# Retention in a two-layer hybrid decoder on one Trainium2 core: the later queries meet the first 256 keys through one state matrix per head

## The chip, the cores and the metric

The kernel runs on one core of one Trainium2 chip. The metric is the device time of one execution in microseconds (us); lower is better. The profile comes from one execution of the same program, recorded by the hardware profiler. The engines are TensorE (PE for its matmuls, PEld for its weight loads), VectorE (DVE), ScalarE (ACT), GpSimd (POOL) and SyncE (SP, which issues most of the DMAs).

## The reference, cut to what matters

Two decoder layers over 16 meta tokens and 512 real ones (T = 528, width 1024). In each layer one projection feeds eight heads of forgetting attention (FoX) of 64 columns and four retention heads of 128. The heads' outputs are concatenated, projected and added to the stream; a SwiGLU block follows. For a retention head:

```python
o_t = sum_{s<=t} gamma_h^(t-s) (q_t.k_s) v_s        # gamma_h = 1 - 2**(-5-h)
q, k = rotate(rq), rotate(rk) * 128**-0.5
y = (o - mean(o)) * rsqrt(var(o) + EPS) * g          # over the head's 128 columns
ret_out = silu(rg) * y
```

The sum over s can be taken key by key, as scores and then products, or for a group of keys at once: the matrix sum_s gamma^(c-s) k_s v_s^T is a state of 128x128, and a query t >= c meets it with the weight gamma^(t-c). Both give the same o.

## The kernel before

Everything is held transposed, 128 features on the partitions and the 528 tokens in the free dimension. Each fp32 operand is split into a high and a low half in the format fp32r (`split`, L149: a copy by ScalarE at L150, a subtraction by VectorE at L151), and each product is three matmuls: high x high, high x low, low x high. In layer 0 all tokens are computed, in layer 1 (`real`) only the queries of the 512 real ones.

A retention head is a list of steps made by `ret_steps` (L671). `values` (L677) transposes the values on TensorE, subtracts each key's mean over the head's columns (so the group norm needs no mean later) and splits them into `rvh`, `rvl`. `scores` (L699) takes a group of key blocks of 128 keys: offsets 0, 128, 256, 384 and a last block of 16 keys at 512. It loads the head's decay table `dec` (128 x 528) once by SyncE (L702, one buffer for all heads), multiplies keys by all queries that come after the block's first key (L722), multiplies the result out of PSUM by the decays (L727, `sd`) and splits it into `rsh`, `rsl`; the block of 16 goes to a small tile `re` (L735 to L737). `product` (L741) multiplies values by scores into one PSUM bank `po` of 512 columns (L756, the block of 16 at L753), in layer 0 the 16 meta columns into a bank of their own (L761, copied at L762); behind the last block ScalarE copies `po` to `d` (L764) and the squares for the norm are taken. `weigh`, `head_norm` and `gate` finish the head; its result `mxh`, `mxl` feeds the output projection.

The groups are {0}, {1} and {2, 3, 4} (L800), so a head has three steps of scores and three of products. Widths of the score matmuls in layer 0: twice 264, 400, 272, 144 and 16 columns; in layer 1: 512, 400, 272, 144 and 16.

The order on TensorE is written out by hand (L1349): the plan is one list of steps, and TensorE executes it in that order. The base of a stretch is the dense projections, one step for each 128 input features (`dense_steps`, L205: six matmuls of 264 columns or three of 512; L225). Between its steps are merged (`merge`, L254) the steps of one pair of attention heads (scores at L519, turns by transposes at L429, products at L589) and those of the retention heads, at places given as numbers of base steps (`ret_places`, L1321, called for heads 0 and 1 each in a stretch of its own, for heads 2 and 3 in one together). With `f` for the list of a head's steps, the ten places go to values, scores of 0, scores of 1, product of 0, scores of 2-4, product of 1, product of 2-4, weigh, norm and gate. The order of the instructions on the other engines follows from a scheduler that goes by the order of the program and by what is ready. The weights of a projection are fetched by SyncE into three buffers (L166) some steps ahead and cast and split by ScalarE with VectorE or GpSimd (L199, L202).

## Time and profile before

| | before |
|---|---|
| device time, median of 3 runs | 1268.74 us (1267.4 to 1270.0) |
| the profiled execution's own time | 1268.53 us |
| its span, first to last instruction | 1266.7 us |
| TensorE busy / its weight loader busy | 1251.2 us (99%) / 1194.1 us (94%) |
| VectorE busy | 991.9 us (78%) |
| ScalarE busy | 704.8 us (56%) |
| GpSimd busy | 273.3 us (22%) |

The span is what the profile covers; the 1.8 us between it and the execution's time lie around it. Busy shares are means over the whole span. Matmuls overlap in the array, so the sum of their durations is no measure of TensorE's time; the distance from one start to the next is. A wait is put down to what came last before the waiting instruction.

### The profile page before, as it was taken

To read this page: it belongs to the slowest core of one execution; us is meant where nothing else is said; L and a number is where in the kernel's file an instruction comes from. 1 tells how busy PE (TensorE), PEld (TensorE's weight loads), DVE (VectorE), ACT (ScalarE), POOL (GpSimd) and SP (SyncE) were. 2 spreads that over 40 slices of the span, in tenths; PEclk is the share of its full clock that TensorE was granted. 3 is DMA by queue.
4 is the path that set the end of the run, shared out by engine and by line. 5 is a ranking of instruction groups with operands and counts; after the bars stand their busy time and mean duration, and the time that the engine had idled before them with its cause. 6 is when DMAs were issued, how large, how long until landed. Compare 5 with 4: busy or idle time off the path is not lost.

```text
span 1266.7 us, 23526 instructions
## 1 busy us (share of the span) xinstructions
PE 1251.2 (99%) x9225; PEld 1194.1 (94%) x9225; DVE 991.9 (78%) x1804; ACT 704.8 (56%) x1301; POOL 273.3 (22%) x539
## 2 busy tenths in 40 slices
PE   9999999999999999999999999999999999999997
PEld 8899999999999999999999989998789999999996
DVE  8887756779988888887786877567899888888867
ACT  6766655676444444444466766557764444444445
POOL 3455546420000000000126556554100000000000
PEclk9999999999999999999999999999999999999999
DMA  6122222223333333332322122222223333333321
GB/s 218 50 76 75 76 77 72 72 67 118 104 97 100 100 101 100 101 101 84 101 77 84 60 86 74 70 90 67 100 94 123 100 101 101 100 101 101 100 84 67
DMA packets 43342, 116.19 MB, mean 92 GB/s; under 512 B 5088, under 2 KB 12000, under 8 KB 43232
## 3 DMA queue, kind: packets, MB, share of 16 engines
q1 hardware_dynamic: 42800, 114.41, 28.1%
q8 instruction: 72, 1.18, 0.4%
q14 instruction: 38, 0.31, 0.1%
q10 hardware_dynamic: 432, 0.29, 0.1%
HBM read 112.58 MB, written 2.10 MB: 91 GB/s over the span
## 4 chain that ended last, share of the span: by engine, by line
PE 93%; ACT 3%; DVE 3%; issue 1%; DMA 0%; ACTq 0%; DVEq 0%
PE psd L225 30%; PE psa L907 18%; PE psd L1042 14%; PE psd L907 13%; PE psa L225 5%; PE psa L1042 4%; PE psa L429 2%; PE psa L519 2%; PE psa L589 1%; PE psa L756 1%; PE psa L722 1%; ACT whi L199 1%; PE psa L298 0%; ACT xh L327 0%; DMA raw<-w_in 0%
## 5 line engine op out<-in xcount | busy, mean ns | idle before, releaser
L202 POOL TENSOR_TENSOR wlo<-raw,whi 128x128 fp32r<-128x128 f32 x504 | 258.2, 548 | 260.1 <-ACT whi L199 259.7
L225 PE MATMUL psd<-xh,whi 128*128 128x264 f32 (+1 forms) x792 | 195.5, 314 | 0.2 <-DVE tq L442 0.2
L225 PE MATMUL psd<-xl,whi 128*128 128x264 f32 (+1 forms) x792 | 186.7, 303 | 0.6 <-DVE xl L328 0.6
L225 PE MATMUL psd<-xh,wlo 128*128 128x264 f32 (+1 forms) x792 | 187.0, 304 | 0.0
L225 PEld LDWEIGHTS psd<-xh,whi 128*128 128x128 f32 x792 | 128.6, 189 | 5.0 <-issue 0.6
L225 PEld LDWEIGHTS psd<-xh,wlo 128*128 128x128 f32 x792 | 127.2, 188 | 6.2 <-DVE wlo L202 0.4
L225 PEld LDWEIGHTS psd<-xl,whi 128*128 128x128 f32 x792 | 127.8, 189 | 5.4 <-DVE xl L328 1.4
L199 ACT CAST whi<-raw 128x512 fp32r<-128x512 f32 (+1 forms) x168 | 97.9, 613 | 41.5 <-PE psd L225 28.4
L895 ACT CAST whi<-raw 128x1024 fp32r<-128x1024 f32 (+2 forms) x62 | 54.9, 885 | 51.3 <-PE psd L907 39.8
L895 ACT CAST fwhi<-raw 128x1024 fp32r<-128x1024 f32 (+2 forms) x62 | 55.6, 897 | 47.5 <-PE psd L907 40.0
L122 POOL MEMSET kc<- 64x528 f32 x2 | 1.1, 533 | 345.4 <-PE psa L907 345.4
L896 DVE TENSOR_TENSOR wlo<-raw,whi 128x1024 fp32r<-128x1024 f32 (+2 forms) x62 | 62.9, 1014 | 12.7 <-ACT whi L895 12.6
L896 DVE TENSOR_TENSOR fwlo<-raw,fwhi 128x1024 fp32r<-128x1024 f32 (+2 forms) x62 | 64.0, 1032 | 11.1 <-ACT fwhi L895 10.9
L907 PE MATMUL psa<-th,whi 128*128 128x264 f32 (+1 forms) x232 | 65.4, 282 | 0.0
L907 PE MATMUL psa<-th,wlo 128*128 128x264 f32 (+1 forms) x232 | 65.4, 282 | 0.0
L907 PE MATMUL psa<-tl,whi 128*128 128x264 f32 (+1 forms) x232 | 65.3, 282 | 0.0
L907 PE MATMUL psa<-th,fwhi 128*128 128x264 f32 (+1 forms) x224 | 63.4, 283 | 0.0
L907 PE MATMUL psa<-tl,fwhi 128*128 128x264 f32 (+1 forms) x224 | 63.3, 283 | 0.0
L907 PE MATMUL psa<-th,fwlo 128*128 128x264 f32 (+1 forms) x224 | 63.2, 282 | 0.0
L536 ACT ACTIVATE pr<-pr,nmax 128x144 f32<-128x144 f32 (+1 forms) x64 | 36.8, 576 | 45.4 <-DVE nmax L523 26.1
L895 ACT CAST fwhi<-S 128x1024 fp32r<-128x1024 f32 x20 | 21.0, 1049 | 68.6 <-PE psa L907 66.5
L973 ACT COPY e<-psa 128x264 f32<-128x264 f32 (+1 forms) x114 | 42.8, 376 | 28.4 <-PE psa L907 24.1
(365 smaller groups left out, 4041.2 us busy)
## 6 DMA issues: line engine op xcount, KB each, us to landing
raw<-w_in SPq DMA_DIRECT2D x54, 512.0 KB, 3.5
raw<-w_gate SPq DMA_DIRECT2D x44, 512.0 KB, 3.9
fraw<-w_up SPq DMA_DIRECT2D x38, 512.0 KB, 3.5
raw<-w_down SPq DMA_DIRECT2D x64, 256.0 KB, 2.9
raw<-w_out SPq DMA_DIRECT2D x16, 512.0 KB, 3.4
raw<-w_down SPq DMA_DIRECT2D x32, 192.0 KB, 2.5
raw<-w_up SPq DMA_DIRECT2D x6, 512.0 KB, 3.5
h<-x_t SPq DMA_DIRECT2D x8, 264.0 KB, 4.5
```

The source lines that it names most:

```text
L199: pin(nc.scalar.copy(hi, job["raw"][:, c0:c1]), pinned)
L202: pin(sub(lo[:, c:c + step], job["raw"][:, c0 + c:c0 + c + step], hi[:, c:c + step].bitcast(F32)), pinned)
L225: nc.tensor.matmul(ps[1][b][:, 0:c1 - c0], w[:, wk, :], x[:, c0:c1], start=(k == 0 and i == 0), stop=(k == n - 1 and i == 2))
L429: nc.tensor.transpose(ps[:, 128 * j:128 * j + 128], src[:, o:o + 128], idt)
L519: nc.tensor.matmul(sc[0:nq, 0:c1 - c0], qq[:, q0:q0 + nq], kk[:, c0:c1], start=(i == 0), stop=(i == 1))
L536: nc.scalar.activation(pr, pr, AF.Exp, bias=nmax[0:nq], scale=-1.0, accum_out=rsum)
L589: nc.tensor.matmul(po[:, c0:SEQ], v[:, j, :], pp[:, j, META + c0:T], start=(j == 0 and i == 0), stop=(j == 4))
L895: nc.scalar.copy(hi, src)
L896: nc.vector.tensor_sub(lo, src, hi.bitcast(F32))
L907: nc.tensor.matmul(bank()[:, 0:b.shape[-1]], a[:, o + k, :], b, start=(fresh and k == 0 and i == 0), stop=(k == n - 1 and i == 2), skip_gr ...
L973: nc.scalar.copy(self.t["e"][:, i], self.t["x"][:, 0:w])
L1042: nc.tensor.matmul(v[:, 0:c1 - c0], a[:, s * n + k, :], b[:, c0:c1], start=(k == 0 and i == 0), stop=(k == n - 1 and i == 2))
```

## The change

Queries from token 256 on (`CUT`) no longer meet key blocks 0 and 1 one by one. `scores` takes blocks 0 and 1 only against queries below 256 (256 and 128 columns; 240 and 128 in layer 1), both in one PSUM bank, and blocks 2 to 4 as before. A new step `keys` transposes the rotated keys of blocks 0 and 1 (kept in fp32 in a tile of their own, `rkf`) on TensorE, weights each key with its decay up to token 256 and splits them. A new step `memory` multiplies them with the centred values to the state, six matmuls of 128 columns, and splits it. `product` of the second group begins with three matmuls of the state by the queries from 256 on (272 columns). The decays in the table for blocks 2 to 4 are now those of the key alone; the query's factor is multiplied on at the end, by VectorE out of PSUM into columns 256 on of `d`, in place of a copy by ScalarE; the first 240 real columns are copied by ScalarE once block 1 is done. A head has ten steps as before, now values, scores of 0-1, keys, memory, scores of 2-4, product of 0-1, product of 2-4, weigh, norm and gate, and they take the same ten places in this order. The decay table is 962 columns wide.

```diff
@@ -33,6 +33,9 @@
 GAMMA = tuple(1.0 - 2.0 ** (-5 - h) for h in range(RH))
 NEG = -1.0e30
 HALF = T // 2
+CUT = 256
+DOFF = (0, 0, CUT, T, 2 * T - CUT - 128)
+DEC = DOFF[4] + META + T - CUT + 2
 PSTEP = 416
 
 
...
@@ -630,13 +633,15 @@
                 nc.scalar.copy(sv(xsw, rl, 0, 64), pv(ps, rl, 64, 128))
                 nc.scalar.copy(sv(xsw, rl, 64, 128), pv(ps, rl, 0, 64))
                 nc.vector.tensor_mul(sv(xsw, rl), sv(xsw, rl), sv(ly["sr"], rl))
-                t1 = tt("tq")
+                t1 = at("rkf", F32) if nm == "rk" else tt("tq")
                 nc.vector.tensor_mul(sv(t1, rl), pv(ps, rl), sv(ly["cr"], rl))
                 nc.vector.tensor_add(sv(t1, rl), sv(t1, rl), sv(xsw, rl))
                 th = at(nm + "h")
                 tl = at(nm + "l")
                 split(sv(th, rl), sv(tl, rl), sv(t1, rl))
                 st[nm] = (th, tl)
+                if nm == "rk":
+                    st["rkf"] = t1
             return go
 
         def v_done(ps):
...
@@ -692,36 +697,32 @@
                     nc.vector.tensor_sub(vh[64:128, 4], c[64:128, 0], vl[64:128, 4].bitcast(F32))
             st["rv"] = (vh, vl)
 
-        def q_start(j):
-            return max(qlo, KOFF[j] if j < 4 else SEQ)
+        def q_range(j):
+            return max(qlo, KOFF[j]), (CUT if KOFF[j] < CUT else T)
 
 
         def scores(grp):
             if grp[0] == 0:
-                dec = at("dec", F32, (128, T), 1)
+                dec = at("dec", F32, (128, DEC), 1)
                 nc.sync.dma_start(dec, decay[hd])
                 st["dec"] = dec
             dec = st["dec"]
             (qh, ql), (kh, kl) = st["rq"], st["rk"]
             sd = tt("sd")
             used = 0
-            ps = None
+            ps = psum_a()
             reads = []
             for j in grp:
-                q0 = q_start(j)
-                d0 = q0 - KOFF[j]
-                n = T - q0
+                q0, q1 = q_range(j)
+                d0 = DOFF[j] + q0 - KOFF[j]
+                n = q1 - q0
                 kn = KLEN[j]
-                for c0, c1 in (((0, HALF), (HALF, n)) if n > 512 else ((0, n),)):
-                    if ps is None or n > 512:
-                        ps = psum_a()
-                    off = used if len(grp) > 1 else 0
-                    sc = ps[0:kn, off:off + c1 - c0]
-                    ko = KOFF[j]
-                    for i, (a, b) in enumerate(((kh, qh), (kh, ql), (kl, qh))):
-                        nc.tensor.matmul(sc, a[:, ko:ko + kn], b[:, q0 + c0:q0 + c1], start=(i == 0), stop=(i == 2))
-                    reads.append((kn, slice(used + c0, used + c1), sc, slice(d0 + c0, d0 + c1)))
-                kept[j] = (used, grp[0])
+                sc = ps[0:kn, used:used + n]
+                ko = KOFF[j]
+                for i, (a, b) in enumerate(((kh, qh), (kh, ql), (kl, qh))):
+                    nc.tensor.matmul(sc, a[:, ko:ko + kn], b[:, q0:q1], start=(i == 0), stop=(i == 2))
+                reads.append((kn, slice(used, used + n), sc, slice(d0, d0 + n)))
+                kept[j] = used
                 used += n
             for kn, o, sc, dd in reads:
                 nc.vector.tensor_mul(sd[0:kn, o], sc, dec[0:kn, dd])
...
@@ -738,30 +739,56 @@
                 kept["e"] = e
             kept["t", grp[0]] = (sh, sl)
 
+        def keys():
+            (_, n, p3), = transpose_into(st["rkf"], KOFF[0:2])
+            th, tl = (at(f"rt{i}", shape=(128, 2, 128)) for i in "hl")
+            for j in range(n):
+                g = st["dec"][:, DEC - 2 + j:DEC - 1 + j]
+                nc.scalar.activation(th[:, j], p3[:, j], AF.Copy, scale=g)
+                nc.vector.scalar_tensor_tensor(tl[:, j], p3[:, j], g, th[:, j].bitcast(F32), ALU.mult, ALU.subtract)
+            st["kt"] = th, tl
+
+        def memory():
+            (th, tl), (vh, vl) = st["kt"], st["rv"]
+            ps = psum_a()[:, 0:128]
+            for j in range(2):
+                for i, (a, b) in enumerate(((th, vh), (th, vl), (tl, vh))):
+                    nc.tensor.matmul(ps, a[:, j, :], b[:, j, :], start=(j == 0 and i == 0), stop=(j == 1 and i == 2))
+            mh, ml = (at(f"rm{i}", shape=(128, 128)) for i in "hl")
+            split(mh, ml, ps)
+            st["memory"] = mh, ml
+
         def product(grp):
             vh, vl = st["rv"]
             if grp[0] == 0:
                 st["po"] = psum_a()
                 st["d"] = at("d", F32, bufs=2)
             po, d = st["po"], st["d"]
+            sh, sl = kept["t", grp[0]]
+            if grp[0]:
+                (mh, ml), (qh, ql) = st["memory"], st["rq"]
+                for i, (a, b) in enumerate(((mh, qh), (mh, ql), (ml, qh))):
+                    nc.tensor.matmul(po[:, CUT - META:SEQ], a, b[:, CUT:T], start=(i == 0), stop=False)
             for j in grp:
-                used, g0 = kept[j]
-                q0 = q_start(j)
+                used = kept[j]
+                q0, q1 = q_range(j)
                 qa = max(q0, META)
-                sh, sl = kept["t", g0]
                 if j == 4:
                     nc.tensor.matmul(po[:, SEQ - META:SEQ], vh[:, 4, :], kept["e"], start=False, stop=True)
                 else:
                     for i, (a, b) in enumerate(((vh, sh), (vh, sl), (vl, sh))):
-                        nc.tensor.matmul(po[:, qa - META:SEQ], a[:, j, :], b[:, used + qa - q0:used + T - q0],
-                                         start=(j == 0 and i == 0), stop=False)
+                        nc.tensor.matmul(po[:, qa - META:q1 - META], a[:, j, :], b[:, used + qa - q0:used + q1 - q0],
+                                         start=(j == 0 and i == 0), stop=(j == 1 and i == 2))
                 if j == 0 and not real:
                     pm = psum_a()
                     for i, (a, b) in enumerate(((vh, sh), (vh, sl), (vl, sh))):
                         nc.tensor.matmul(pm[:, 0:META], a[:, 0, :], b[:, 0:META], start=(i == 0), stop=(i == 2))
                     nc.scalar.copy(d[:, 0:META], pm[:, 0:META])
+                if j == 1:
+                    nc.scalar.copy(d[:, META:CUT], po[:, 0:CUT - META])
                 if j == 4:
-                    nc.scalar.copy(d[:, META:T], po)
+                    with tc.high_priority():
+                        nc.vector.tensor_mul(d[:, CUT:T], po[:, CUT - META:SEQ], st["dec"][:, DEC - 2 - T + CUT:DEC - 2])
                     sq = tt("sq")
                     if hd == RH - 1:
                         sh, sl = tt("sqh", F32R), tt("sql", F32R)
...
@@ -797,8 +824,9 @@
             split(sv(mh, real), sv(ml, real), sv(d, real))
             st["mix"] = (mh, ml)
 
-        G = ((0,), (1,), (2, 3, 4))
-        return [values] + [lambda g=g: scores(g) for g in G] + [lambda g=g: product(g) for g in G] + [weigh, head_norm, gate]
+        G = ((0, 1), (2, 3, 4))
+        return [values, lambda: scores(G[0]), keys, memory, lambda: scores(G[1]),
+                lambda: product(G[0]), lambda: product(G[1]), weigh, head_norm, gate]
 
     def add_h(m, real):
         def go(ps):
...
@@ -1320,8 +1348,7 @@
 
         def ret_places(hd, *places):
 
-            f = rs[hd]
-            return list(zip(places, (f[0], f[1], f[2], f[4], f[3], f[5], f[6], f[7], f[8], f[9])))
+            return list(zip(places, rs[hd]))
 
         for g in range(2):
             main, rest = fs[g]
...
@@ -1356,12 +1383,17 @@
     ang = np.arange(T, dtype=np.float32)[None, :] * inv[:, None]
     cos, sin = np.cos(ang), np.sin(ang)
     rope = np.stack([np.concatenate([cos, cos], 0), np.concatenate([-sin, sin], 0)]).astype(np.float32)
-    decay = np.zeros((RH, 128, T), np.float64)
+    decay = np.zeros((RH, 128, DEC), np.float64)
     k = np.arange(128)[:, None]
-    q = np.arange(T)[None, :]
     for hd in range(RH):
-        decay[hd] = np.where(q >= k, np.exp(np.maximum(q - k, 0) * math.log(GAMMA[hd])), 0.0)
-    decay = (decay * 128.0 ** -0.5).astype(np.float32)
+        g = math.log(GAMMA[hd])
+        for o, n, base in ((0, CUT, None), (DOFF[2], T - CUT, 0), (DOFF[3], T - CUT - 128, 128), (DOFF[4], META, CUT)):
+            q = np.arange(n)[None, :]
+            power = q - k if base is None else 0 * q - k - base
+            decay[hd][:, o:o + n] = np.where(q >= k, np.exp(np.where(q >= k, power, 0) * g), 0.0) * 128.0 ** -0.5
+        decay[hd][:, DOFF[4] + META:DEC - 2] = np.exp(np.arange(T - CUT)[None, :] * g)
+        decay[hd][:, DEC - 2:] = np.exp((CUT - np.array([[0, 128]]) - k) * g) * 128.0 ** -0.5
+    decay = decay.astype(np.float32)
     mask = np.where(np.arange(128)[None, :] <= np.arange(128)[:, None], 0.0, NEG).astype(np.float32)
     return rope, decay, mask, np.eye(128, dtype=np.float32)
 
```

## Prediction

> **What bounds the kernel now.** I read the page first, then the waits of TensorE and of its weight loader, then the timeline around each retention head, engine by engine.
>
> ```profile
> span 1266.7 us, 23526 instructions
> ...
> PE 1251.2 (99%) x9225; PEld 1194.1 (94%) x9225; DVE 991.9 (78%) x1804; ACT 704.8 (56%) x1301; POOL 273.3 (22%) x539
> ...
> PE 93%; ACT 3%; DVE 3%; issue 1%; DMA 0%; ACTq 0%; DVEq 0%
> ```
>
> TensorE is busy for 99% of the span, its weight loader for 94%, and the chain that ended last is 93% TensorE. So the change is worth what it does to TensorE's stream of instructions, plus what it adds to or takes from TensorE's waits. The retention heads cause few of these:
>
> ```profile
> PE psa L756 <- DVE rsl L151: 0.7, 2, 0.4
> PEld psa L756 <- DVE rsl L151: 1.6, 3, 0.7
> ```
>
> Both rows tell of the same stalls, in which a product waits for the low half of its scores: between 0.7 and 1.6 us, and I take 1.2.
>
> What a matmul costs is not its duration (they overlap) but the distance from its start to the next start:
>
> ```profile
> 215.17 0.28 PE L722 MATMUL psa<-rqh,rkh 128*128 128x264 f32 x1
> ...
> 215.90 0.41 PE L225 MATMUL psd<-xh,whi 128*128 128x264 f32 x2
> ...
> 217.06 0.34 PE L722 MATMUL psa<-rql,rkh 128*128 128x400 f32 x1
> ...
> 217.42 0.40 PE L225 MATMUL psd<-xh,whi 128*128 128x264 f32 x2
> ...
> 220.38 0.29 PE L722 MATMUL psa<-rqh,rkh 128*128 128x272 f32 x1
> ...
> 220.76 0.23 PE L722 MATMUL psa<-rqh,rkh 128*128 128x144 f32 x1
> 220.82 0.28 PE L722 MATMUL psa<-rql,rkh 128*128 128x144 f32 x1
> ```
> ```profile
> 864.77 0.39 PE L722 MATMUL psa<-rqh,rkh 128*128 128x512 f32 x1
> 865.00 0.40 PE L722 MATMUL psa<-rql,rkh 128*128 128x512 f32 x1
> ...
> 872.09 0.71 PE L429 MATMUL psa<-idt,pd 128*128 128x128 f32 x5
> 872.55 0.48 PE L225 MATMUL psd<-xh,whi 128*128 128x512 f32 x1
> 872.87 0.39 PE L225 MATMUL psd<-xl,whi 128*128 128x512 f32 x1
> ```
> ```profile
> 1248.24 0.27 PE L907 MATMUL psa<-ah,whi 128*128 128x240 f32 x1
> ...
> 1249.92 0.28 PE L907 MATMUL psa<-ah,whi 128*128 128x240 f32 x1
> ```
>
> 512 columns take 0.23 us. 400 take 0.36/2 = 0.18, 272 take 0.38/3 = 0.127, 264 take 0.73/6 = 0.122, and 240 take 1.68/15 = 0.112. I put 256 between the last two, at 0.118. Five transposes of 128 columns take 0.46 us, and the matmul behind them takes 0.32 instead of 0.23, so they cost (0.46 + 0.09)/5 = 0.11 each. From 240 columns down to 128 the price hardly falls: below that width I read the loading of a fresh 128x128 weight as the limit. This decides the sum.
>
> **The change, part by part.**
>
> *TensorE's stream, for one head.* Scores of the first two key blocks: in layer 0 they were six matmuls of 264 and three of 400 (6 x 0.122 + 3 x 0.18 = 1.27 us) and become three of 256 and three of 128 (0.35 + 0.33 = 0.68), a gain of 0.59. In layer 1 three of 512 and three of 400 (1.23) become three of 240 and three of 128 (0.67), a gain of 0.56. Products: three of 512 and three of 400 (1.23) become three of 240, three of 128 and three of 272 against the state (0.34 + 0.33 + 0.38 = 1.05), a gain of 0.18. New: two transposes of the keys and six matmuls of 128 columns for the state, 8 x 0.11 = 0.88 us. Key blocks 2, 3 and 4 keep their widths. Net: 0.88 - 0.77 = +0.11 us in layer 0 and 0.88 - 0.74 = +0.14 in layer 1; over four heads each, **+1.0 us** (the last digit of the rows leaves some 0.4 either way). A third of the score columns go, yet the stream gets no shorter, since what goes is wide and what comes is narrow.
>
> [...]
>
> *A wait of the second product.* Accumulator `po` is one bank of 512 columns. The new `product` copies its columns 0 to 240 out on ScalarE after key block 1, and the state's matmuls then write columns 240 to 512 of the same bank. Does TensorE wait for that copy, though the columns differ? The trace has two like cases:
>
> ```profile
> 128.16 0.17 PE L722 MATMUL psa<-rqh,rkl 128*16 128x16 f32 x1
> ```
> ```profile
> 127.53 0.69 DVE L151 TENSOR_TENSOR ptl<-psa,pth 128x512 fp32r<-128x512 f32 x1
> 128.37 0.72 DVE L727 TENSOR_TENSOR sd<-psa,dec 128x272 f32<-128x272 f32 x3
> ```
> ```profile
> L500 ACT CAST vv<-psa 128x256 fp32r<-128x256 f32 x16 | 5.9, 369 | 5.2 <-PE psa L429 2.5 <-DVE vv L501 2.5
> ```
>
> VectorE was free at 128.22 but began on the 272 columns of block 2 only at 128.37, when the 16 columns of block 4 in that bank were done (128.16 + 0.17). And ScalarE's copies at L500 sat idle 2.5 us for VectorE's reads of other columns of their bank. So the program orders accesses by bank, and I expect TensorE's second product, with everything behind it in TensorE's queue (the next projection), to wait for ScalarE's copy. No row here shows TensorE itself waiting for a reader.
>
> [...]
>
> How long? The second product would start about 0.3 us ahead of the old last product (the head has by then saved 0.3, mainly keys for scores). The first product's last matmul lands one projection step before that in heads 1 and 3, two steps before in head 0 (a step is six matmuls of 264, 0.73 us), over two in head 2. Then the copy must find ScalarE free, and takes 0.37 (the 256-column row above). The old last products began at:
>
> ```profile
> 79.17 0.29 PE L756 MATMUL psa<-rsh,rvh 128*128 128x272 f32 x1
> ...
> 134.72 0.29 PE L756 MATMUL psa<-rsh,rvh 128*128 128x272 f32 x1
> ...
> 259.20 0.29 PE L756 MATMUL psa<-rsh,rvh 128*128 128x272 f32 x1
> ...
> 709.95 0.29 PE L756 MATMUL psa<-rsh,rvh 128*128 128x272 f32 x1
> ...
> 763.72 0.29 PE L756 MATMUL psa<-rsh,rvh 128*128 128x272 f32 x1
> ...
> 883.07 0.39 PE L756 MATMUL psa<-rsh,rvh 128*128 128x272 f32 x1
> ```
>
> These are heads 0, 1, 3 of layer 0, then of layer 1. What ScalarE is then still doing:
>
> ```profile
> 78.27 0.63 ACT L449 CAST qs<-tq 64x528 fp32r<-64x528 f32 x1
> ...
> 133.58 0.63 ACT L449 CAST qs<-tq 64x528 fp32r<-64x528 f32 x1
> ...
> 258.54 0.63 ACT L150 CAST mxh<-mixt 128x528 fp32r<-128x528 f32 x1
> ...
> 709.10 0.61 ACT L449 CAST qs<-tq 64x512 fp32r<-64x512 f32 x1
> ...
> 762.71 0.61 ACT L449 CAST qs<-tq 64x512 fp32r<-64x512 f32 x1
> ...
> 855.58 0.63 ACT L536 ACTIVATE pr<-pr,nmax 128x400 f32<-128x400 f32 x1 [1.52 <-DVE nmax L523]
> ...
> 882.92 0.62 ACT L150 CAST mxh<-mixt 128x512 fp32r<-128x512 f32 x1
> ```
>
> I put the copy behind these casts, since ScalarE takes its instructions in the order of the program as far as they are ready. Head 3 of layer 1: cast done at 883.54, copy at 883.9, product wanted at 882.8: 1.1 us. Head 3 of layer 0: 259.17 + 0.37 against 258.9: 0.6. Head 1: 134.21 + 0.37 against 134.4, and 763.32 + 0.37 against 763.4: 0.2 and 0.3. Head 0: 78.90 + 0.37 against 78.9, and 709.71 + 0.37 against 709.6: 0.4 and 0.5. Head 2 has ScalarE idle (1.52 us ahead of 855.58): nothing. Together **+3.1 us**. From below the bound is nothing (a copy ahead of the casts); from above 1.1 in all eight heads, 8.8. I take 3.1, nearest to the rows.
>
> *The keys and the state.* Both halves of the turned keys are cut out of one bank by ScalarE and VectorE in turn, four steps by these rows:
>
> ```profile
> L150 ACT CAST pth<-psa 128x128 fp32r<-128x128 f32 x16 | 4.2, 262 | 1.0 <-PE psa L429 0.8
> L151 DVE TENSOR_TENSOR ptl<-psa,pth 128x128 fp32r<-128x128 f32 x16 | 4.4, 277 | 0.3
> ```
>
> That is 2 x (0.26 + 0.28) = 1.1 us without any queue. In head 0 the state's matmuls follow two steps (1.5 us) and some turns of attention behind the keys, in the others four steps or more. I charge head 0 0.3 us in layer 0 and 0.4 in layer 1, **+0.7 us**; at least nothing, at most the 1.1 twice. The state's own split (two such steps) has two steps or more to hide in, and in head 3 it queues beside the copy charged above. The old stalls, **-1.2 us**, sat at products that now start with other operands or later.
>
> *ScalarE and VectorE.* Scores shrink by 544 columns a head in a multiply, a copy and a subtraction, and 256 + 128 columns of keys and state and the 272-column multiply on `po` come in, with as many instructions as go. At 56% and 78% busy they are covered by TensorE: nothing. If that cover went, it would show in the waits above.
>
> *The load of the decay table.* It grows from 528 to 962 columns, and the buffer now comes free only after the last product's multiply.
>
> ```profile
> SPq L702 <- DVE sd L727: 24.9, 6, 5.9
> ...
> 856.52 8.45 SPq L166 DMA_DIRECT2D raw<-w_out  x2
> ```
>
> SyncE waits there already, 24.9 us in six times, and it will wait some 6 us longer each time, with the next weight load queued behind. At head 3 of layer 1 that load came at 856.52 anyway, just when the multiply will be done (products end near 856.3). Weights are fetched steps ahead: nothing; a late weight would cost what is left of the 6 us.
>
> **Sum**, against the profiled execution's own 1268.53 us (span 1266.7; the median is 1268.74, so it stands for it): 1268.5 + 1.0 + 3.1 + 0.7 - 1.2 = **1272.1 us**.
>
> **Rivals.**
> - *The waits hide.* ScalarE makes the copies early, and the new waits merely replace the old 1.2 us: 1268.5 + 1.0 = 1269.5. For it speaks ScalarE's 56%; against it the casts that stand at each place.
> - *The waits spread.* The order on ScalarE puts every head where head 3 of layer 1 is: 8 x 1.1 + 0.7 - 1.2 + 1.0 = +9.3, 1277.8. Against it: head 2's idle ScalarE.
> - *Narrow is cheap* (the other side). If loads run ahead while wide matmuls stream, a narrow one costs its columns alone. The first of the 144-column ones above cost 0.06 (220.76 to 220.82). With fourteen narrow ones a head, 14 x 0.05 x 8 = 5.6 us less and the waits hidden: 1268.5 + 1.0 - 5.6 = 1263.9. It decides once most narrow ones, not the first of a run, go at 0.06. [...]
>
> **How the numbers follow.** Forecast 0.58 (its own range 1270.4 to 1274.2), waits hidden 0.24, waits spread 0.10, narrow cheap 0.08. About 0.2%, 2.5 us, is what a measurement of this kernel can tell from no change. Above 1271.3 lie 0.46 of the forecast's 0.58 and all of the spread case: slower 0.56. The rest of the forecast and the hidden case: same 0.36. Faster 0.08. The range 1268.6 to 1276.0 holds forecast and hidden case and leaves out the fast case and most of the spread one.
>
> **What would show it.** Right: 128-column matmuls at 0.11 us from start to start in the state; TensorE waiting at the state's product for ScalarE's copy of `d`, longest in head 3; weights never late. Wrong: narrow ones at 0.06, no wait at the second product, or TensorE waiting for a weight behind the decay table.

## The result, and the profile after

The changed kernel takes 1287.94 us (median of 5 runs, 1284.36 to 1289.79) against 1268.74 us before: 1.0138 times as long, 95% interval 1.0123 to 1.0154. Forecast were 1272.1 us in a range to 1276.0. The sign was right; the loss is 18 to 19 us and not 3.6.

The page of the changed kernel (its profiled run took 1287.94 us) has these lines for those of before:

```profile
span 1285.8 us, 23724 instructions
...
PE 1260.4 (98%) x9301; PEld 1202.1 (93%) x9301; DVE 993.0 (77%) x1824; ACT 704.9 (55%) x1317; POOL 275.4 (21%) x539
...
PE 89%; DVE 5%; ACT 5%; issue 1%; DMA 0%; DVEq 0%; ACTq 0%
```

TensorE's part of the last chain fell from 93% to 89%, VectorE's and ScalarE's rose from 3% to 5% each. The waits of TensorE and of its weight loader in the changed kernel (engine, line, who ended the wait: us in all, times, longest):

```profile
PE psa L771 <- ACT d L788: 5.6, 6, 1.8
...
PE psa L756 <- DVE rsl L154: 2.1, 1, 2.1
...
PE psa L723 <- DVE rkl L154: 1.4, 1, 1.4
PE psa L785 <- DVE mixt L596: 0.8, 1, 0.8
```
```profile
PEld psa L771 <- ACT d L788: 7.1, 6, 2.0
...
PEld psa L756 <- ACT rth L747: 3.6, 3, 2.4
```

L771 is the first matmul of the second product (state times queries), L788 ScalarE's copy of the first product into `d`: the wait that was forecast at 3.1 us is there, at 5.6 or 7.1. L756 is now the state's own matmuls: 3.6 us in the loader's row, forecast at 0.7. Before, the largest row of the retention heads was the 1.6 us of `rsl`.

Not forecast at all is what the next view shows, the table by stretches, first of the kernel before and then of the changed one. Its columns are the stretch and its length, the busy time (and instructions) of PE, PEld, DVE, ACT and POOL, the granted clock, the DMA share and GB/s.

```profile
72.70:79.50 6.80, 6.80 (x57) 6.71 (x56) 5.42 (x12) 5.51 (x12) 2.06 (x4) 1.00 0.14 40
...
714.40:717.80 3.40, 3.40 (x28) 3.31 (x27) 3.33 (x6) 3.32 (x6) 2.65 (x4) 1.00 0.16 59
```
```profile
69.30:72.70 3.40, 1.25 (x11) 1.04 (x9) 1.77 (x6) 3.39 (x10) 0.00 (x0) 1.00 0.43 154
72.70:79.50 6.80, 6.66 (x32) 6.36 (x32) 3.06 (x11) 1.78 (x5) 0.00 (x0) 0.50 0.00 0
...
711.00:714.40 3.40, 2.56 (x13) 1.67 (x12) 2.11 (x5) 2.37 (x7) 0.82 (x2) 1.00 0.35 131
714.40:717.80 3.40, 3.40 (x18) 3.00 (x17) 1.40 (x4) 0.63 (x2) 0.00 (x0) 0.50 0.06 23
```

In head 0 of both layers TensorE's clock is halved for 6.8 and 3.4 us, right behind a stretch in which TensorE was idle for 2.15 and 0.84 us. (Both kernels also have a stretch of 3.4 us at half clock at 42 us, ahead of the heads: 0.50 from 41.67 to 45.08 us before, from 41.99 to 45.40 after.) TensorE is "busy" in the halved stretches (6.66 of 6.80 us, 3.40 of 3.40), so neither the busy share nor the list of waits shows their cost. The timeline does:

```profile
76.74 0.43 PE L723 MATMUL psa<-rql,rkh 128*128 128x272 f32 x1
76.97 0.43 PE L723 MATMUL psa<-rqh,rkl 128*128 128x272 f32 x1
```

272 columns take 0.23 us from start to start, where they took 0.127.

**Where the 19.1 us went** (the difference of the two spans). I laid the two traces side by side by the projection matmuls, which are the same in both. TensorE's stream, each matmul priced by its width, is 0.7 us longer. Second product: 7.1. State in head 0: the last projection matmul ahead of it starts at 69.94 and the next behind it at 74.23; less that matmul's 0.24 and the state's own 6 x 0.11, 3.4 us; in layer 1 (711.43 to 713.98, by 0.23 and 0.66) 1.7. Half clock, an estimate: half of 6.8 and 3.4, some 0.6 of it already counted in the 3.4: 4.5. Together 17.4. The other 1.7 are single waits in heads 1 and 3 (`rkl` 1.4, `mixt` 0.8 and smaller ones), less the old stalls.

### The profile page after: what moved, and what is told of

It is laid out like the page before. It is cut to its first block, busy times and chain, and to the rows that moved or that the text cites. A ratio compares the mean times of both kernels' runs of the same rounds, so it can differ in the third digit from the quotient of the medians.

```text
span 1285.8 us, 23724 instructions
## 1 busy us (share of the span) xinstructions
PE 1260.4 (98%) x9301; PEld 1202.1 (93%) x9301; DVE 993.0 (77%) x1824; ACT 704.9 (55%) x1317; POOL 275.4 (21%) x539
## 4 chain that ended last, share of the span: by engine, by line
PE 89%; DVE 5%; ACT 5%; issue 1%; DMA 0%; DVEq 0%; ACTq 0%
PE psd L228 28%; PE psa L935 18%; PE psd L1070 14%; PE psd L935 13%; PE psa L228 5%; PE psa L1070 4%; PE psa L432 2%; PE psa L522 1%; PE psa L592 1%; ACT whi L202 1%; PE psa L723 1%; PE psa L392 1%; PE psa L780 1%; ACT qo L452 0%; PE psa L771 0%
```

## The experiments

Theories, named in the expectations by letter: **A**: the program orders accesses by PSUM bank, TensorE idles, and the clock halves behind the idle time. **B**: VectorE and ScalarE are late as a whole, and a wait taken away returns at the next place. **C**: the clock goes with the head's matmuls, not with waiting. **D**: the clock goes by columns streamed. **E**: one slow clamp on VectorE makes head 0 late. Ratios are to the kernel before, measured beside each run; a thousandth is 1.3 us.

### The second product's wait: bank, order or place

**Own bank** (e1_own_bank):

```diff
+            o = META
             if grp[0]:
+                po, o = psum_a(), CUT
...
-                    nc.tensor.matmul(po[:, CUT - META:SEQ], a, b[:, CUT:T], start=(i == 0), stop=False)
+                    nc.tensor.matmul(po[:, 0:T - CUT], a, b[:, CUT:T], start=(i == 0), stop=False)
```

> The second product gets a PSUM tile of its own; everything else is the changed kernel. Theory A (the program orders accesses by bank, so TensorE waits at the second product for ScalarE's copy of d): the rows of TensorE at the second product waiting for that copy go, and with them 6 to 7 us of the changed kernel's 1287.9: 1281 to 1282. The two stretches of half clock in head 0 and the state's waits stay. Rival B (ScalarE and VectorE are behind in these places, and TensorE meets their lateness wherever it needs them): the wait only moves, to the second product's wait for the low half of its scores or to the ring of four PSUM tiles, and the time stays within 2 us of 1287.9.

1282.16 us, ratio 1.0090 (1.0076 to 1.0103): 6 us less than the changed kernel. The loader's rows of the second product are now:

```profile
PEld psa L773 <- DVE rml L154: 1.1, 2, 0.6
PEld psa L773 <- ACT rmh L153: 0.9, 1, 0.9
```

The row of `d` is gone; 2.0 us of waiting for the state's halves stood behind it. Of the two halvings in head 0 that of layer 0 stayed; that of layer 1 was not there this time (mean granted clock 0.72 from 70 to 82 us, 1.00 from 712 to 726). So the wait needs the shared bank, though the columns that ScalarE reads and TensorE writes differ. Rival B falls here.

**Copy first** (e6_copy_first):

```diff
-                    nc.scalar.copy(d[:, META:CUT], po[:, 0:CUT - META])
+                    with tc.high_priority():
+                        nc.scalar.copy(d[:, META:CUT], po[:, 0:CUT - META])
```

> The changed kernel, with its one PSUM tile for both products; only the copy of d is given priority on ScalarE. Theory A (the wait at the second product is long because the copy stands behind ScalarE's casts of mixt and of the queries, which themselves wait for VectorE): the wait of 7.1 us in all shrinks to 1 to 2 us, about 5 to 6 us less than 1287.9: 1282 to 1283, close to the run with a tile of its own. Rival (the wait is the length of the copy itself, or its matmuls end late): it stays at 6 to 7 us, and so does the time, within 2 us.

1288.64 us, ratio 1.0143 (1.0127 to 1.0159), and the wait as it was. But the experiment did not make what it was to test: ScalarE's order in head 0 of layer 0 is that of the changed kernel, with the copy still behind the cast of `mixt`:

```profile
85.72 0.63 ACT L153 CAST mxh<-mixt 128x528 fp32r<-128x528 f32 x1 [0.57 <-DVE mixt L602]
86.26 0.35 ACT L789 COPY d<-psa 128x240 f32<-128x240 f32 x1
```

So it tells nothing of the order's part. Its rows show why the wait is long all the same: ScalarE idles for VectorE's `mixt`, casts it, and only then copies. The copy's input is there earlier: in head 0 of layer 0 of the changed kernel the first product ends at 83.21 us (82.94 + 0.27), and its copy begins at 85.34. The changed kernel has the same in layer 1, with TensorE behind it:

```profile
723.74 0.62 ACT L153 CAST mxh<-mixt 128x512 fp32r<-128x512 f32 x1 [0.65 <-DVE mixt L602]
724.26 0.35 ACT L788 COPY d<-psa 128x240 f32<-128x240 f32 x1
...
724.67 0.39 PE L771 MATMUL psa<-rqh,rmh 128*128 128x272 f32 x1 [1.55 <-ACT d L788]
```

**Second product later** (e16_second_later): one bank, but the second product is placed two steps later in heads 0, 1 and 3. The ten places are those of the values, first scores, keys, state, second scores, first product, second product, weighing, norm and gate.

```diff
-  head 0: (13, 33.5, 35.5, 37.5, 39, 40.5, 43, 44, 47.5, 48)
+  head 0: (13, 33.5, 35.5, 37.5, 39, 40.5, 45, 45.1, 47.5, 48)
-  head 1: (13, 33.5, 35.5, 39.5, 39, 41.5, 43, 44, 47.5, 48)
+  head 1: (13, 33.5, 35.5, 39.5, 39, 41.5, 45, 45.1, 47.5, 48)
-  ret_places(3, 52, 45.5, 47.5, 57.5, 55.5, 58.5, 60, 64.1, 63, 64.2)
+  ret_places(3, 52, 45.5, 47.5, 57.5, 55.5, 58.5, 62, 64.1, 63, 64.2)
```

> The changed kernel with its one PSUM tile for both products; only the place of the second product moves, two projection steps (1.5 us) later in heads 0, 1 and 3. Theory A (the wait there ends with ScalarE's copy of d, which is late behind casts but not later than 2 us): the wait of 7.1 us shrinks below 1.5 us, and the time falls by about as much as with a tile of its own, 5 to 6 us: 1282 to 1283, with the copy on ScalarE where it was. Rival (moving the second product only moves what is late: the copy of d stays one step behind whatever TensorE does): the wait stays above 4 us, 1286 to 1289.

1283.8 us, ratio 1.0106 (1.0091 to 1.0122): 4 us less. TensorE's waits:

```profile
PE psa L301 <- ACT sqh L796: 0.9, 2, 0.5
...
PE psa L301 <- DVE sql L798: 0.7, 2, 0.4
...
PE psa L771 <- ACT d L788: 0.6, 2, 0.3
```

The wait for `d` went from 5.6 to 0.6 with the bank still shared, so it takes both: one bank, and a copy that comes up to 2 us too late for it. A part came back one step on, where TensorE sums the squares of `d` (L301), as the rival said. The half clock of 6.8 us in head 0 of layer 0 stayed (mean granted clock 0.72 from 70 to 82 us).

### The state in head 0, and the clock

**State later** (e2_state_later):

```diff
-  head 0: (13, 33.5, 35.5, 37.5, 39, 40.5, 43, 44, 47.5, 48)
+  head 0: (13, 33.5, 35.5, 39.4, 39, 40.5, 43, 44, 47.5, 48)
```

> Only the place of the state's matmuls in head 0 is changed: from two projection steps behind the keys to four, behind the second scores. Theory A (TensorE waits there for the keys' halves, and the granted clock halves right behind that idle time): in both layers the wait of 2.3 and 0.8 us and most of the small ones behind it (1.3 us) go, and the stretches of half clock (6.8 and 3.4 us, which cost half their length) go too: 8 to 10 us less, 1278 to 1280. Rival C (the half clock comes with the many narrow matmuls of the changed head, not with the wait): only the 3 to 4 us of waiting go, 1284 to 1285, and the stretches of half clock stand in head 0 as before. Rival B (VectorE late): the wait moves to the second product, within 2 us of 1287.9.

1286.03 us, ratio 1.0118 (1.0101 to 1.0134): 2.5 us less, where 8 to 10 were expected, and by time alone not told from none, since its interval and the changed kernel's overlap. Both waits of the state went, and neither of the halvings of head 0 behind them is there (in layer 0 the granted clock is 1.00 from 70 to 82 us). But:

```profile
PE psa L771 <- ACT d L788: 6.9, 6, 3.0
...
PE psa L723 <- DVE ptl L154: 1.4, 1, 1.4
PE psa L780 <- DVE mixt L587: 1.1, 1, 1.1
```

TensorE now came earlier to the things that were late anyway. The longest wait for `d`, in head 0 of layer 1, grew from 1.8 to 3.0 us, and from that wait on the clock was halved for 6.8 us; 272 columns take 0.23 us there:

```profile
721.53 0.60 PE L771 MATMUL psa<-rqh,rmh 128*128 128x272 f32 x1 [2.98 <-ACT d L788]
...
722.61 0.43 PE L780 MATMUL psa<-rsl,rvh 128*128 128x272 f32 x1
722.84 0.43 PE L780 MATMUL psa<-rsh,rvl 128*128 128x272 f32 x1
```

It was halved for 3.4 us more in head 1 of layer 0, behind the waits of 0.8 us for `mixt` and 0.3 for `d` at its products. Rival C falls, since the halvings moved with the waits; rival B holds in part.

**Fillers** (e4_filler); what they compute is overwritten:

```diff
-            ps = psum_a()[:, 0:128]
+            ps = psum_a()
+            for _ in range((9, 4)[l] if hd == 0 else 0):
+                nc.tensor.matmul(ps, ones, vh[:, 0:4], start=True, stop=True)
+            ps = ps[:, 0:128]
```

> The state stays two steps behind the keys, but in head 0 TensorE first does nine (layer 0) and four (layer 1) matmuls of 512 columns into the state's PSUM tile, whose sums are overwritten: 3.0 us of work that computes nothing. Theory A (idle time of TensorE halves the clock): the fillers take the place of the waits of 2.3 and 0.8 us, so the work is about free, and the two stretches of half clock go: 4 to 5 us less than 1287.9, 1283 to 1284, faster though it does more. Rival C (the clock goes with the head's narrow matmuls, or comes on its own): the half clock stays where it was, and the time is 1288 to 1289.

1286.08 us, ratio 1.0127 (1.0112 to 1.0142), 1.4 us less with overlapping intervals: by time alone, unclear. The trace tells more. The two halvings of head 0 are gone though 3 us of work were added in their place; two others of 3.4 us appeared in head 1: in layer 0 behind the 0.8 us for `mixt` and 0.3 for `d`, in layer 1 behind 1.8 us for `d`. The changed kernel had these waits too, without a halving. So behind such a wait the clock halved in one execution and not in another; the mean granted clock is 0.993 in this execution and 0.996 in the other three.

**Narrow fill** (e10_narrow_fill), on the kernel with own bank and later state, whose heads had no half clock:

```diff
+            n = (64, 128)[l]
+            for _ in range(64 if hd == 2 else 0):
+                nc.tensor.matmul(ps[:, 0:n], ones, vh[:, 0, 0:n], start=True, stop=True)
```

> The kernel with own tile and later state (which showed no half clock in the heads) with 64 useless matmuls ahead of the state in head 2: of 64 columns in layer 0, of 128 columns in layer 1. Both should take 0.11 us each, so that TensorE is equally busy by its records: 14 us more. Theory D (the clock of a stretch of 3.41 us goes by the columns streamed in the stretch before it: in the six traces so far the halved stretches follow at most 3030 columns, the full ones at least 3260): 64-column matmuls stream about 2000 in a stretch and 128-column ones about 4000, so the clock halves after the fill of layer 0 and not after that of layer 1: 1293 to 1296. Rival A (idle time alone decides): no half clock at either, 1291 to 1292.

This is the table by stretches: two rows from the fill of layer 0 on, then the fill of layer 1 and the stretch behind it; below it the timeline's rows of the two fills and of the matmul behind the second.

```profile
229.50:234.30 4.80, 4.80 (x46) 4.80 (x45) 2.63 (x5) 2.71 (x6) 4.15 (x8) 1.00 0.00 0
234.30:247.90 13.60, 13.60 (x65) 13.60 (x65) 0.66 (x2) 1.38 (x4) 0.21 (x1) 0.50 0.13 40
...
873.00:880.00 7.00, 7.00 (x66) 7.00 (x64) 2.35 (x4) 2.29 (x4) 4.32 (x8) 1.00 0.14 36
880.00:887.00 7.00, 7.00 (x60) 7.00 (x60) 1.92 (x5) 2.02 (x6) 0.00 (x0) 1.00 0.10 42
```
```profile
229.44 9.26 PE L756 MATMUL psa<-rvh,ones 128*128 128x64 f32 x64
...
872.79 7.26 PE L756 MATMUL psa<-rvh,ones 128*128 128x128 f32 x64
879.88 0.28 PE L759 MATMUL psa<-rvh,rth 128*128 128x128 f32 x1
```

TensorE was never idle in either fill, and the clock halved for 13.6 us behind the 64-column matmuls and not at all behind the 128-column ones, whose distance is (879.88 - 872.79)/64 = 0.111 us. Theory A's second half (idle time) falls as the only cause, and D stands: what went with the halving is the columns streamed. It is one execution, and the two fills lie in different layers. The halving lasted two stretches longer than I had expected (1298.72 us in all against an expected 1293 to 1296): at half clock the same work streams fewer columns in a stretch, and the first three such stretches had 1024, 2544 and 3000.

**Clamp on ScalarE** (e11_clamp_on_act, on the changed kernel; e13_before_clamp, the same edit on the kernel before):

```diff
-            nc.vector.tensor_scalar_max(u, x, -80.0)
-            nc.scalar.activation(u, u, AF.Exp, scale=-1.0)
+            nc.scalar.activation(u, x, AF.Relu, bias=c80)
+            nc.scalar.activation(u, u, AF.Exp, scale=-1.0, bias=c80)
```

The occasion was this in the changed kernel, head 0 of layer 0 (VectorE's clamp, GpSimd's weight halves, the keys' halves, the state):

```profile
65.04 3.56 POOL L205 TENSOR_TENSOR wlo<-raw,whi 128x128 fp32r<-128x128 f32 x8
65.26 3.03 DVE L664 TENSOR_SCALAR ge<-sg 128x528 f32<-128x528 f32 x1
...
72.07 0.37 ACT L747 ACTIVATE rth<-psa,dec 128x128 fp32r<-128x128 f32 x1
72.49 0.33 PE L756 MATMUL psa<-rvh,rth 128*128 128x128 f32 x1 [2.15 <-DVE rsl L154]
72.74 0.34 DVE L748 SCALAR_TENSOR_TENSOR rtl<-psa,dec,rth 128x128 fp32r<-128x128 f32 x1
73.11 0.37 ACT L747 ACTIVATE rth<-psa,dec 128x128 fp32r<-128x128 f32 x1 [0.19 <-DVE rtl L748]
73.58 0.33 DVE L748 SCALAR_TENSOR_TENSOR rtl<-psa,dec,rth 128x128 fp32r<-128x128 f32 x1
```

The page names `rsl` as the state's releaser; but the state reads `rth`, written at 72.07 + 0.37, just ahead of 72.49.

> The changed kernel, with one edit: the clamp of the gate in heads 0 and 1 (ge from sg) is done by ScalarE instead of VectorE. In head 0 of layer 0 that clamp took 3.03 us on VectorE, beside GpSimd's eight subtractions, in place of 0.53 us in the kernel before. Theory E (this clamp makes VectorE 2.5 us late, so the keys' halves come late, and the state's wait of 2.3 us and the half clock behind it in head 0 of layer 0 follow from it): the wait there shrinks below 1 us and the half clock of 6.8 us behind it goes: 4 to 6 us less than 1287.9, 1282 to 1284. Rival (the state stands too close behind the keys whatever VectorE does): the wait stays over 1.5 us, with the half clock, 1287 to 1289.

1284.44 us, ratio 1.0107 (1.0091 to 1.0122): some 4 us less. In head 0 of layer 0 the halving behind the state shrank from 6.8 to 3.4 us, the wait only to 1.4:

```profile
PE psa L758 <- ACT rth L749: 2.0, 2, 1.4
```

Half of each theory: the clamp made it worse, and the state also stands too close behind the keys. In layer 1, where the clamp took 0.41 us on VectorE, the wait stayed at 0.6 us; the half clock of layer 1 was missing in this trace, as it was with the own bank and with the second product later.

> The kernel before, unchanged, for a second trace of it: does the clamp in head 0 of layer 0 take 0.53 us again or 3.0 us? If 3.0, then the slow clamp belongs to no kernel, and what differs is that the kernel before has slack behind it; the wait for the low half of the scores in head 0 would then be near 2 us in this trace in place of 0.7. If 0.53, the two traces of before stand against nine of ten traces of changed kernels.

A second trace of the kernel before (e14_before_again, no edit), at 1270.24 us, has the slow clamp too. This is the clamp in the first trace, and then the second one:

```profile
65.49 0.53 DVE L659 TENSOR_SCALAR ge<-sg 128x528 f32<-128x528 f32 x1
```
```profile
65.20 3.04 DVE L659 TENSOR_SCALAR ge<-sg 128x528 f32<-128x528 f32 x1
...
72.00 0.71 DVE L151 TENSOR_TENSOR rsl<-sd,rsh 128x528 fp32r<-128x528 f32 x1 [0.69 <-ACT rsh L150]
...
72.76 0.50 PE L756 MATMUL psa<-rsl,rvh 128*128 128x512 f32 x1 [0.24 <-DVE rsl L151]
```

So the slow clamp belongs to no kernel: of twelve traces with the clamp on VectorE ten show 3.03 or 3.04 us and two (the first trace of before, and own bank with later state) 0.53. Against the first trace, the second one loses 2.2 us between 68 and 74 us of the span, in several small waits, and no half clock follows (mean granted clock 0.997 over this trace). The wait for the low half of the scores, expected near 2 us, was 0.24.

> The kernel before with the clamp on ScalarE and nothing else. If the slow clamp is a matter of the changed kernel alone, nothing changes: 1268.5 to 1271. If the kernel before has it too in some executions (its times lie at 1268.2 to 1268.7 and at 1270.4 to 1273.1), the upper group goes: 1267 to 1269, with less spread.

1269.77 us, ratio 0.9992 (0.9983 to 1.0001): at most a gain of 2 us, and not told from none. The upper group of times did not go: they spread from 1267.7 to 1271.1.

### Everything together

**Own bank and later state** (e3_both, both edits above):

> Own PSUM tile for the second product and the later state in head 0 together. Theory A: the two are independent and add: 6 to 7 and 8 to 10 us less, 1271 to 1274, which leaves 2 to 5 us over the kernel before (1.0 of the stream, the rest waits in heads 1 and 3). Rival B: no more than the larger of the two, 1278 or above.

1277.4 us, ratio 1.0051 (1.0038 to 1.0064), 11 us less than the changed kernel; alone the two gave 6 and 2.5. The clock accounts for the rest in these traces: half of the time at half clock in the heads is 5.1 us in the changed kernel, 3.4 and 5.1 with one edit, and nothing with both, where neither kind of wait is left (mean granted clock 0.997, against 0.993 in the changed kernel and with either edit alone). It still stood 3 us above the expected 1274.

**Without the small bank** (e8_no_small_bank), on top of that:

```diff
-                if j == 0 and not real:
-                    pm = psum_a()
-                    for i, (a, b) in enumerate(((vh, sh), (vh, sl), (vl, sh))):
-                        nc.tensor.matmul(pm[:, 0:META], a[:, 0, :], b[:, 0:META], start=(i == 0), stop=(i == 2))
-                    nc.scalar.copy(d[:, 0:META], pm[:, 0:META])
...
-                    nc.scalar.copy(d[:, META:CUT], po[:, 0:CUT - META])
+                    nc.scalar.copy(d[:, qlo:CUT], po[:, qlo:CUT])
...
-  head 3: (52, 45.5, 47.5, 57.5, 55.5, 58.5, 60, 64.1, 63, 64.2)
+  head 3: (52, 45.5, 47.5, 55.4, 55.5, 58.5, 60, 64.1, 63, 64.2)
...
+                with tc.high_priority() if nm == "rk" and hd == 3 else ExitStack():
+                    split(sv(th, rl), sv(tl, rl), sv(t1, rl))
```

> On top of the own tile and the later state: the first product writes all of tokens 0 to 255 into its own tile, so the separate 16-column product with a PSUM tile of its own goes (layer 0); in head 3 the split of the keys gets priority and the state's matmuls come two steps earlier. Theory A (what is left over the kernel before is single waits, each with its own cause: the ring of four PSUM tiles 1.9 us, the low half of the keys 1.6 us, the state's low half in head 3 1.0 us, and 0.6 us of small matmuls): 5 us less than 1277.4, 1272 to 1273. Rival B (VectorE is late as a whole, and a wait removed comes back at the next thing that TensorE needs): 1275 or more.

1273.95 us, ratio 1.0027 (1.0018 to 1.0037): 3 us less than with both, 5 expected. The long wait for `rkl` (1.4) and that at the small bank (0.8) went. In head 0 of layer 0 its trace has waits of 1.4 us for `ptl` and 1.1 for `mixt`. They are not the price of the edit: the trace of the run with both edits has the quick clamp, and the narrow fill, the same kernel with fills and the slow clamp, has both waits.

**Wide state** (e9_wide_state), on top of that: two matmuls of 256 columns and two of 128 in place of six of 128.

```diff
+                nc.tensor.matmul(ps[:, 0:256], th[:, j, :], st["v2"][:, :, j, :], start=(j == 0), stop=False)
+                nc.tensor.matmul(ps[:, 0:128], tl[:, j, :], vh[:, j, :], start=False, stop=(j == 1))
...
+            nc.scalar.copy(m, ps[:, 128:256])
+            nc.vector.tensor_add(m, ps[:, 0:128], m)
```

> As the run without the small bank, and the state is made of two matmuls of 256 columns (high halves of the keys against both halves of the values side by side) and two of 128, in place of six of 128, with one copy and one addition more ahead of its split. Theory A (a 128-column matmul costs 0.11 us and a 256-column one 0.118, and the rest is hidden by early placing): 8 x 0.2 = 1.6 us less than the run without the small bank, about 1271, within 0.2% of the kernel before. Rival: the longer way from the state to its halves makes the second product wait, 0.5 us or more in heads 0 and 1, and nothing is gained.

1275.26 us, ratio 1.0036 (1.0022 to 1.0050): no gain, as its rival said. The longer way shows at the second product (L779), which waits 1.0 us in all for the state's halves in head 0 and head 1 of layer 1, and at the first product, where 1.1 us became 1.5 in head 0 and 0.4 in head 1 of layer 0:

```profile
PE psa L788 <- DVE sq L761: 1.9, 2, 1.5
```

**All cures** (e12_best): the kernel without the small bank, with the clamp on ScalarE.

> The run without the small bank (own tile, later state, no 16-column product, split of the keys first and state earlier in head 3), with the clamp on ScalarE. Theory E: the two waits left in head 0 of layer 0 (1.5 us at the second scores, 1.3 us at the first product) go or shrink: 2 to 3 us less than 1273.95, 1271 to 1272, within 0.2% of the kernel before. Rival: these waits come from the ring of four PSUM tiles alone, and the time stays at 1273 to 1275.

1272.42 us, ratio 1.0020 (1.0012 to 1.0029), the lowest time of the change that I found, and still 2.5 us slower than before. The clamp's own part in it is not shown: the interval overlaps that of the run without the small bank. Priced by width, TensorE's stream is within half a microsecond of before's; the waits left are single ones:

```profile
PEld psa L785 <- DVE mixt L589: 1.3, 1, 1.3
PEld psa L303 <- DVE sql L798: 1.3, 2, 0.7
PEld psa L726 <- DVE ptl L156: 0.8, 1, 0.8
```

**Products earlier** (e15_products_earlier), on top of all cures:

```diff
-  head 0: (..., 39.4, 39, 40.5, 43, ...)    head 1: (..., 39.5, 39, 41.5, 43, ...)    head 3: (..., 55.4, 55.5, 58.5, 60, ...)
+  head 0: (..., 39.4, 39, 40.5, 42, ...)    head 1: (..., 39, 38.5, 40.5, 42, ...)    head 3: (..., 55, 54.5, 57.5, 59, ...)
```

> The best run so far (1272.4, ratio 1.0020) with the second products of heads 0 and 1 one step earlier, in head 1 the scores, state and first product as well, and in head 3 the products one step earlier. If the 4.5 us of waiting that it still has over the kernel before are lateness behind the second product (sums of squares waited for at 717 and 891 us), 1 to 2 us go: 1270.5 to 1271.5, level with the kernel before. If they are lateness ahead of it (mixt and the keys' halves on VectorE), earlier places cost 1 us or more: 1273 to 1275.

1274.6 us, ratio 1.0034 (1.0021 to 1.0046): no better, if anything worse. Whether the last 2.5 us can be won by another order I leave open; nothing here beat the kernel before.

## Why the prediction was wrong, point by point

Between the forecast's 3.6 us and the 19.1 between the two traces lie 15.5. The second product's wait has 4.0 of them, the state's 4.4, the half clock 4.5, the waits in place of the old stalls 2.9; the stream came out 0.3 lower.

- **TensorE's stream, +1.0.** Right: +0.7. The state's matmuls go at 0.11 us, as the five transposes had said. That the loading of a weight sets this price is my reading; what the narrow fill shows is that at full clock 46 matmuls, all but two or so of 64 columns, are counted in 4.80 us (0.10 to 0.11 each), against 0.111 for 128 columns, with the loader busy for all of both stretches (4.80 of 4.80 us, 7.00 of 7.00). In head 3 of layer 1 of the changed kernel it is 0.33 us from the start of one to the start of the third behind it:

```profile
898.71 0.27 PE L756 MATMUL psa<-rvl,rth 128*128 128x128 f32 x1
...
899.04 0.27 PE L756 MATMUL psa<-rvl,rth 128*128 128x128 f32 x1
```

- **The second product's wait, +3.1.** The mechanism was right (bank, not columns; own bank removes it, as that run shows), and so was head 2 at nothing; the size was 7.1 by the loader's row. I put the copy behind the casts that ScalarE had *at that time in the trace of before*, and took those casts to be ready. In heads 0 and 1 it stood behind another one, that of `mixt`, for which ScalarE first idles 0.57 to 0.75 us; it did not go by what was ready, since in head 0 of layer 0 the copy's input was there at 83.21 us and the copy began at 85.34. There I had 0.2 to 0.5 us a head; 1.2 (head 0) and 0.5 (head 1) came in layer 0, and 1.8 and 2.0 in layer 1. Heads 3, where I had 0.6 and 1.1, gave 0.5 and 1.1. So the sign "longest in head 3" was wrong: the longest wait is head 1's of layer 1.
- **The keys and the state, +0.7.** This step failed. "0.3 us in layer 0 and 0.4 in layer 1", at most "the 1.1 twice": 3.4 and 1.7 us came. The chain of four steps through one bank was rightly seen. But the place two steps behind the keys was priced with VectorE as punctual as in the one trace of before, and that trace was one of the two out of twelve in which the clamp took 0.53 and not 3.03 us. This explains layer 0 in part: with the clamp on ScalarE 1.4 of the 2.15 us of idling ahead of the state were still there. In layer 1 the 1.7 us came with a quick clamp. With the state four steps behind the keys both waits went.
- **The clock, not in the sum.** I charged idle time at its own length. Behind it came 10.2 us at half clock, 4.5 us of loss that no row of waits contains. The kernel before has full clock in its heads, and I took that for given. The narrow matmuls play a part here that I had not seen either: a stretch with 128-column matmuls (0.111 us each) streams about half as many columns as one with projections (264 columns in 0.122), and so needs less idle time to come down to the counts behind which the clock was halved (1576 to 3072 columns in 3.413 us).
- **The old stalls, -1.2.** They went, but waits of the same kind took their place at the scores (`rkl`, 1.4) and at the ring of four PSUM tiles (`mixt`, 0.8), where I had put ScalarE and VectorE at nothing ("covered by TensorE").
- **The decay table's load, nothing.** Right: no wait for `dec` is among the changed kernel's rows, and the loader's waits for halves of a weight are 0.4 and 0.2 us, against 0.4 before. But SyncE's wait at the table did not grow by some 6 us each time: it fell from 24.9 to 8.0 us in six times.
- **The rivals.** "The waits spread" (1.1 us in every head) was nearest in time with 1277.8, but not in kind: the waits stayed uneven, from 0 in head 2 to 2.0. "Narrow is cheap" fell with the 0.11 us, "the waits hide" with the 7.1.

## What to carry to other kernels

A new wait of the busiest engine has to be priced with its queue of today and with the lateness of an average execution, not with one trace in which everything was on time: the second trace of before shows the 2.5 us. In this kernel waits of 2.15 and 0.84 us beside narrow matmuls went with 6.8 and 3.4 us of half clock, which cost 3.4 and 1.7 us more by the same estimate; so where TensorE streams without a gap, look for each new place at the columns that it will stream in the 3.4 us around it. And in this program accesses of two engines to one PSUM bank are ordered even at different columns (the 5.6 us for `d`), so a reader in the middle of an accumulator's life wants a bank of its own, or a step or two more of distance.

## What the runs showed of the hardware

- **The clock went with the columns streamed.** In each trace the starts of the halved stretches lie on one grid of 3.413 us (72.71 and 714.41 in the changed kernel are 188 steps apart). I added up the columns of the matmuls that start in each step of that grid, from 50 us on to 10 us before the end, in the sixteen traces of this case. The twelve halvings follow steps with 1576 to 3072 columns. Of 5649 steps at full clock that were followed by full clock three had 3072 or fewer (2864, 3056, 3072), and the median had 7392. (The 3030 and 3260 in the narrow fill's expectation are 3072 and 3264 by this count.) So there is no sharp mark, and in the last 10 us, where TensorE runs out of work, the count does not decide: in four traces a step with 1920 to 2640 columns was followed by full clock. The grid does not lie alike against the program: counted back in steps, it begins 0.71 us behind the span's start in the trace of before and 1.03 in that of the changed kernel (from the halvings at 41.67 and 41.99 us). So a wait can fall into one step or be shared by two, and I infer from this why halvings come and go between executions. That they also make the changed kernel's spread of 5 us is no more than inferred either, but its five runs fit it: mean granted clocks of 0.995 at 1284.36 and 1286.26 us, 0.993 at 1287.94 and 1289.79, and 0.992 at 1289.27. A gap of 2.15 us stood ahead of one halving, one of 0.84 us ahead of another, and with 64-column matmuls there was no gap at all.
- **The clamp beside GpSimd's subtractions.** The same clamp took 0.53 or 3.03 us beside GpSimd's run of eight subtractions (3.56 to 3.57 us long), begun 0.22 us behind their start in the quick and in the slow case alike (65.49 behind 65.27 us in the first trace of before, 65.26 behind 65.04 in the changed kernel). In layer 1 of the changed kernel it took 0.41 us (512 columns), begun at 708.98 within such a run of 3.70 us from 708.12 on. What makes it slow is not shown by any run here, nor why two traces of twelve escape.
